# Token rows kept in plain feature order, and every eighth feature taken as stationary columns on TensorE

## The chip, the core and the metric

The kernel runs on one core of a Trainium2 chip. The metric is the device time of one execution in microseconds (us); lower is better. The engines are TensorE (PE in the profile; its weight loads have a row of their own, PEld), VectorE (DVE), ScalarE (ACT), GpSimd (POOL) and SyncE (SP), which issues most of the DMAs.

## The reference

The model has two layers over 256 tokens of `x` and, in layer 0, 256 tokens of context as well, with 1024 features. Each layer is a mixer (two kinds of attention in layer 0, one in layer 1) with its output projection, a residual and layer norm, then a mixture of 16 experts, of which every token takes 2, and another residual and layer norm.

```python
x = layer_norm(ALPHA * x + g1 * y, ln_g[l, 0], ln_b[l, 0])
h2 = x * (1.0 + sc2) + sh2
x = layer_norm(ALPHA * x + g2 * moe(h2, ...), ln_g[l, 1], ln_b[l, 1])

def moe(h, w_router, b_router, w_gate, w_up, w_down):
    scores = jax.nn.sigmoid(h @ w_router)
    ...                                   # best of 4 groups, its 2 best experts, gates
    g = jnp.einsum('...d,edf->...ef', h, w_gate)
    u = jnp.einsum('...d,edf->...ef', h, w_up)
    a = jax.nn.silu(g) * u * gates[..., None].astype(h.dtype)
    return jnp.einsum('...ef,efd->...d', a, w_down)
```

`w_gate` and `w_up` have 1024 x 512 values per expert, `w_down` 512 x 1024. All of it is fp32.

## The kernel before

Tokens lie in tiles of 128 partitions: four tiles in layer 0 (two of `x`, two of context), two in layer 1. `out_proj` closes each mixer. For every tile it multiplies the attention output with the output weights (L855), adds the residual on VectorE (L857, L858), takes the statistics for the layer norm, and computes the router's logits on TensorE (L872, L877). The reciprocal root of the variance is a power on GpSimd (`rstd`, L370). Two VectorE instructions then make the row `h2` that the experts see: one subtracts the mean and multiplies with a row (L887), the other multiplies with the reciprocal root and adds a row (L894). The scores are made beside them (L890, L891, L893, L901, L902). Behind the last tile the routing begins (`route_a`, `route_b`), a long chain of small VectorE instructions.

The feature order matters because of the expert weights. `w_gate` and `w_up` are loaded so that partition p holds the features 8p to 8p + 7, in eight slices k; slice k of the weights therefore holds every eighth feature, starting with k. The transposed tokens that are multiplied with slice k must hold the same features. Before the change `h2` is written in that order: L887 reads its inputs in order and writes feature 8q + k to column 128k + q, and L894 reads and writes in that permuted order. Neighbouring elements of the write are thus 512 bytes apart.

Layer 0: `h2` is stored to `h2d` in DRAM by a DMA on ScalarE's queue (L897). For each block of 128, 64 or 32 tokens of an expert, GpSimd gathers rows into `xg` (L1207) and `xgT` transposes them on TensorE, eight transposes for the eight slices of 128 columns. In a transpose the data is the stationary operand, loaded by a weight load, and the identity is the moving one; `tr` is the helper of all transposes (L234). VectorE or ScalarE copies the result to `xt` (L1223), `products` multiplies it with gate and up weights (L1232, L1234 for 128 tokens, L1247 for fewer), `hidden` makes the activation, `down` the down product (L1284, L1290). There are 20 blocks, so 160 transposes.

Layer 1: `h2` stays in SBUF as `h2s`, split into two fp32r parts, the cast (L899, ScalarE) and what the cast leaves (L900, VectorE). `pick` takes the tokens of a group of blocks out of it with one-hot matrices `ddr`: for each of eight slices, two tiles and two parts one matmul with 128 columns of `h2s` as the stationary operand and up to 128 one-hot columns as the moving one (L1311); ScalarE copies the result (L1313). There are seven groups, so 7 x 8 x 2 x 2 = 224 such matmuls.

Expert weights come through rings of buffers on SyncE's queue (L155), each load waiting until its buffer is free.

Of the kernel before, what the change touches and what calls it, by code (L numbers as in the profile page):

```python
# [14 lines left out]
ALU = mybir.AluOpType  # L15
# [6 lines left out]
P = 128  # L22
# [120 lines left out]
class K:  # L143
# [698 lines left out]
    def out_proj(self, l, ts, w, oT, rows, h2d, score):  # L842
        nc, wk = self.nc, self.wkb
        for n, t in [(n, t) for n in range(2) for t in ts]:
            c = t // 2
            g1, G2, B2 = [rows[:, 3 * c + i] for i in range(3)]
            cs = slice(512 * n, 512 * n + 512)
            zs = []
            if n:
                zs.append(self.half_T(self.xs[:, t, 0:512], 0))  # L850
                bs = self.sm.tile([P, 2, 6], F32, name="bs", tag="bs")
                nc.vector.bn_stats(bs[:, 0], self.xs[:, t, 0:512])
            ps = self.psum([P, 512], "acc")
            for k in range(8):
                mm = nc.tensor.matmul(ps, oT[:, k, P * t:P * t + P], w[n](k), start=k == 0, stop=k == 7)  # L855
            y = wk.tile([P, 512], F32, name="y", tag="yw")
            nc.vector.tensor_mul(y, ps, g1[:, cs])  # L857
            nc.vector.scalar_tensor_tensor(self.xs[:, t, cs], self.xs[:, t, cs], ALPHA if l == 0 else 1.0, y,  # L858
                                           op0=ALU.mult, op1=ALU.add)
            if n == 0:  # L860
                continue

            last = t == ts[-1]
            if last:
                w0 = self.warm(7, "m", mm.ins.name)
            zs.append(self.half_T(self.xs[:, t, 512:1024], 1))
            nc.vector.bn_stats(bs[:, 1], self.xs[:, t, 512:1024])
            wg, bl = self.router
            pr = self.psum([P, P], "tr")
            for k in range(8):  # L870
                j = k % 4
                nc.tensor.matmul(pr[32 * j:32 * j + 32, :], wg[:, c, k, :], zs[k // 4][:, j, :], start=k < 4, stop=k > 3,  # L872
                                 tile_position=(0, 32 * j), skip_group_check=True)
            lp = wk.tile([P, P], F32, name="lp", tag="lp", bufs=1)
            nc.scalar.copy(lp, pr)
            ps = self.psum([P, NE], "tr")
            self.routed = nc.tensor.matmul(ps, lp, self.const("sum4"), start=True, stop=True).ins.name  # L877
            mv = self.sm.tile([P, 6], F32, name="mv5", tag="mv5")
            nc.vector.bn_aggr(mv[:, 0:2], bs)
            self.rstd(mv[:, 2:3], mv[:, 1:2], 1, 1e-5)  # L880
            nc.vector.tensor_scalar(mv[:, 3:4], mv[:, 0:1], -1.0, None, op0=ALU.mult)

            z = self.xs[:, t, :]
            h2 = wk.tile([P, D], F32, name="h2", tag="h2")

            hq, rq = "p (k q) -> p q k", "p (q k) -> p q k"
            nc.vector.scalar_tensor_tensor(h2.rearrange(hq, k=8), z.rearrange(rq, k=8), mv[:, 0:1], G2.rearrange(rq, k=8),  # L887
                                           op0=ALU.subtract, op1=ALU.mult)
            sc = score[:, t, :]
            nc.vector.scalar_tensor_tensor(sc, bl[:, c, 1], mv[:, 3:4], ps, op0=ALU.mult, op1=ALU.add)  # L890
            nc.vector.scalar_tensor_tensor(sc, sc, mv[:, 2:3], bl[:, c, 0], op0=ALU.mult, op1=ALU.add)  # L891

            e = nc.scalar.activation(sc, sc, AF.Exp, scale=-1.0)  # L893
            nc.vector.scalar_tensor_tensor(h2.rearrange(hq, k=8), h2.rearrange(hq, k=8), mv[:, 2:3], B2.rearrange(rq, k=8),  # L894
                                           op0=ALU.mult, op1=ALU.add)
            if l == 0:
                nc.scalar.dma_start(h2d[P * t:P * t + P, :], h2)  # L897
            else:
                nc.scalar.copy(self.h2s[0][:, t], h2)  # L899
                nc.vector.tensor_sub(self.h2s[1][:, t], h2, self.h2s[0][:, t])  # L900
            nc.vector.tensor_scalar(sc, sc, 1.0, None, op0=ALU.add)  # L901
            nc.vector.reciprocal(sc, sc)  # L902
            nc.vector.tensor_mul(mv[:, 4:5], mv[:, 3:4], mv[:, 2:3])
            nc.scalar.activation(z, z, AF.Identity, scale=mv[:, 2:3], bias=mv[:, 4:5])
            if last:
                i = nc.scalar.activation(self.junk, self.nhalf[:, 0:1], AF.Sigmoid)
                self.tc.add_manual_dep(i.ins, e.ins.name, NOSYNC, reason="behind the exponentials")
# [302 lines left out]
    def scatter(self, y, si, R, yd, NT):  # L1210
        nj = P // R
        self.nc.gpsimd.indirect_dma_start(out=yd.rearrange("r (j w) -> (r j) w", j=nj), out_offset=IOA(ap=si, axis=0),
                                          in_=y, in_offset=None, bounds_check=2 * NT * nj - 1, oob_is_err=False)

    def xgT(self, xg, R):
        nc = self.nc
        xt = self.ep.tile([P, 8, R], F32, name="xt", tag="xt")
        kb = min(8, 512 // R)
        for k0 in range(0, 8, kb):
            pt = self.psum([P, kb, R], "tr")  # L1220
            for k in range(kb):
                self.tr(pt[:, k, :], xg[:R, P * (k0 + k):P * (k0 + k) + P], R)
            nc.any.tensor_copy(xt[:, k0:k0 + kb, :], pt)  # L1223
        return xt

# [72 lines left out]
    def pick(self, dd, T):  # L1298

        nc = self.nc  # L1300
        R = dd.shape[2]
        xt = self.ep.tile([P, 8, R], F32, name="xt", tag="xt")
        kb = min(8, 512 // R)
        for k0 in range(0, 8, kb):
            n = min(kb, 8 - k0)
            pt = self.psum([P, n, R], "tr")
            for k in range(n):
                ks = slice(P * (k0 + k), P * (k0 + k) + P)
                for t in range(T):
                    for i in range(2):  # L1310
                        nc.tensor.matmul(pt[:, k, :], self.h2s[i][:, t, ks], dd[:, t, :],  # L1311
                                         start=t == 0 and i == 0, stop=t == T - 1 and i == 1)
            nc.any.tensor_copy(xt[:, k0:k0 + n, :], pt)  # L1313
        return xt
# [572 lines left out]
```

## Time and profile before

| what | us |
|---|---|
| median of three runs | 1063.53 |
| their range | 1056.98 to 1065.07 |
| the profiled execution | 1061.43 |
| its span in the trace | 1059.6 |

The span is the time from the first to the last recorded instruction of the profiled execution; what lies around it makes the difference to that execution's time. An engine's busy time says how long it had work, not whether that work decided the end. Of TensorE the trace shows two rows, the weight loads (PEld) and the matmuls (PE); a load can run while the matmul ahead of it still runs. Waits are read from the idle time ahead of an instruction and from what released it.

### The profile page before, as it was taken

The numbers are of one execution on the slowest core, as the hardware profiler recorded it, in microseconds if no ns is written. First come the engines' busy times: TensorE is split into PE (matmuls) and PEld (weight loads), VectorE is DVE, ScalarE is ACT, GpSimd is POOL, SyncE is SP. The second block draws the span as 40 slices with busy tenths as digits, with TensorE's granted clock in tenths as the row PEclk, the third lists the DMA queues.
The fourth block names the chain that finished last, engine by engine and source line by source line (L and its number), as shares of the span: only waits on it lengthen the run. The fifth ranks groups of instructions, "written<-read, shape, count | busy, mean of one in ns | idle before, by whom it ended". The sixth has DMA issues, their size and how long they took to land. (4 is left out here: it accounts for less than half of the span.)

```text
span 1059.6 us, 15578 instructions
## 1 busy us (share of the span) xinstructions
PE 979.2 (92%) x5918; PEld 533.2 (50%) x5918; DVE 507.3 (48%) x1368; ACT 259.9 (25%) x685; POOL 86.0 (8%) x90
## 2 busy tenths in 40 slices
PE   4799999989899899999999997998999999999994
PEld 1466557667544444544444443443653665544542
DVE  2524555665747833331100105879838742533346
ACT  2433343553412111101111211423413111111110
POOL 0000000000102303111111110111003000000001
PEclk9799999999999999999999899999999889999997
DMA  8899761201265199997999986769634692999991
GB/s 313 298 350 330 258 214 58 80 24 57 105 239 214 63 392 401 408 414 292 390 402 401 358 301 248 315 245 405 263 140 136 252 418 79 417 418 376 363 353 47
DMA packets 76937, 286.99 MB, mean 271 GB/s; under 512 B 12449, under 2 KB 27441, under 8 KB 55604
## 3 DMA queue, kind: packets, MB, share of 16 engines
q1 hardware_dynamic: 71600, 268.13, 65.4%
q0 software_dynamic: 4272, 15.08, 4.0%
q10 hardware_dynamic: 980, 2.66, 0.6%
q8 instruction: 51, 0.84, 0.3%
q14 instruction: 34, 0.28, 0.1%
HBM read 279.77 MB, written 8.69 MB: 272 GB/s over the span
## 5 line engine op out<-in xcount | busy, mean ns | idle before, releaser
L1247 PE MATMUL acc<-wring,xt 128*32 128x256 f32 (+1 forms) x1440 | 140.2, 436 | 0.5 <-ACT xt L1223 0.5
L1247 PEld LDWEIGHTS acc<-wring,xt 128*32 128x32 f32 (+1 forms) x1440 | 59.0, 118 | 73.1 <-issue 49.7
L855 PE MATMUL acc<-wring,oT 128*128 128x512 f32 x192 | 89.2, 598 | 0.3 <-DVE y L857 0.3
L1290 PE MATMUL acc<-wring,aT 128*32 128x256 f32 (+1 forms) x720 | 70.7, 436 | 6.5 <-DVE aT L1272 4.2
L459 PE MATMUL acc<-swh,hT 128*128 128x384 f32 x192 | 68.2, 355 | 3.9 <-ACT v L581 3.5
L460 PE MATMUL acc<-swl,hT 128*128 128x384 f32 x192 | 67.6, 352 | 0.0
L1349 DVE TENSOR_TENSOR xs<-xs,c 128x512 f32<-128x512 f32 x60 | 40.4, 684 | 54.6 <-PE c L1346 54.5
L461 PE MATMUL acc<-swh,hT 128*128 128x384 f32 x192 | 66.2, 345 | 0.0
L523 PE MATMUL acc<-wring,hT 128*128 128x512 f32 x128 | 58.8, 593 | 0.0
L1284 PE MATMUL acc<-wring,aT 128*128 128x512 f32 x128 | 57.1, 597 | 0.5 <-DVE aT L1261 0.4
L1232 PE MATMUL acc<-wring,xt 128*128 128x512 f32 x128 | 56.7, 596 | 0.0
L1234 PE MATMUL acc<-wring,xt 128*128 128x512 f32 x128 | 56.2, 592 | 0.0
L410 PE MATMUL m<-wring,cT 128*32 128x512 f32 x256 | 44.3, 660 | 12.4 <-DMA wring<-in_w_mod_dram 12.4
L855 PEld LDWEIGHTS acc<-wring,oT 128*128 128x128 f32 x192 | 33.9, 190 | 33.0 <-issue 31.4
L1290 PEld LDWEIGHTS acc<-wring,aT 128*32 128x32 f32 (+1 forms) x720 | 27.8, 117 | 38.1 <-issue 20.7
L370 POOL TENSOR_TENSOR mv<-ve,nhalf 128x1 f32<-128x1 f32 x12 | 18.3, 1529 | 330.9 <-DVE ve L369 263.6
L1250 ACT COPY gu<-acc 128x256 f32<-128x256 f32 (+1 forms) x27 | 12.0, 444 | 122.5 <-PE acc L1247 122.5
L459 PEld LDWEIGHTS acc<-swh,hT 128*128 128x128 f32 x192 | 36.4, 189 | 9.5 <-issue 4.5
L1234 PEld LDWEIGHTS acc<-wring,xt 128*128 128x128 f32 x128 | 24.3, 190 | 30.6 <-issue 30.4
L1232 PEld LDWEIGHTS acc<-wring,xt 128*128 128x128 f32 x128 | 23.8, 190 | 28.3 <-issue 27.6
L461 PEld LDWEIGHTS acc<-swh,hT 128*128 128x128 f32 x192 | 36.3, 189 | 3.0 <-issue 3.0
L460 PEld LDWEIGHTS acc<-swl,hT 128*128 128x128 f32 x192 | 36.4, 190 | 2.4 <-issue 2.4
(354 smaller groups left out, 1527.9 us busy)
## 6 DMA issues: line engine op xcount, KB each, us to landing
wring<-in_w_gate_dram SPq DMA_DIRECT2D x58, 1024.0 KB, 14.4
wring<-in_w_up_dram SPq DMA_DIRECT2D x58, 1024.0 KB, 15.3
wring<-in_w_down_dram SPq DMA_DIRECT2D x58, 1024.0 KB, 14.2
wring<-in_w_mod_dram SPq DMA_DIRECT2D x48, 1024.0 KB, 8.1
wring<-in_w_in_even_dram SPq DMA_DIRECT2D x24, 256.0 KB, 4.4
wring<-in_w_in_odd_dram SPq DMA_DIRECT2D x6, 1024.0 KB, 11.4
wring<-in_w_out_even_dram SPq DMA_DIRECT2D x4, 1024.0 KB, 5.1
wring<-yd SPq DMA_DIRECT2D x4, 1024.0 KB, 5.8
```

The costliest lines, as they stand in the source:

```text
L410: nc.tensor.matmul(ps[32 * j:32 * j + 32, :], lhs(k), w[k][:, 512 * j:512 * j + 512], start=k == 0, stop=k == len(w) - 1, tile_position=(0 ...
L459: mm(ps, xh, wh, start=first, stop=False)
L460: mm(ps, xh, wl, start=False, stop=False)
L461: mm(ps, xl, wh, start=False, stop=last)
L523: self.nc.tensor.matmul(ps, h[:, k, :], w(k), start=k == 0, stop=k == 7)
L855: mm = nc.tensor.matmul(ps, oT[:, k, P * t:P * t + P], w[n](k), start=k == 0, stop=k == 7)
L1232: nc.tensor.matmul(pg, xt[:, k, :], gate(k), start=k == 0, stop=k == 7)
L1234: nc.tensor.matmul(pu, xt[:, k, :], up(k), start=k == 0, stop=k == 7)
L1247: nc.tensor.matmul(ps[R * j:R * j + R, :], xt[:, k, :], src[:, W * jj:W * jj + W], start=k == 0, stop=k == 7, tile_position=(0, R * j), sk ...
L1284: nc.tensor.matmul(ps, aT[:, k, :], w(k)[:, 512 * n:512 * n + 512], start=k == 0, stop=k == 3)
L1290: self.last_mm = nc.tensor.matmul(ps[R * j:R * j + R, :], aT[:, k, :], w(k)[:, W * j:W * j + W], start=k == 0, stop=k == 3, tile_position= ...
L1349: nc.vector.tensor_add(x, x, ps)
```

## The change

`h2` is now written in plain feature order: the two VectorE instructions of each tile read and write side by side. The features are picked where the rows go into TensorE: a new helper `eighth` views a row as 128 groups of eight and takes the k-th of each, and `xgT` and `pick` use this view as their stationary operand. Its columns stand eight elements (32 bytes) apart instead of side by side. What comes out of the transposes and picks is the same as before, in the same place.

```diff
-            hq, rq = "p (k q) -> p q k", "p (q k) -> p q k"
-            nc.vector.scalar_tensor_tensor(h2.rearrange(hq, k=8), z.rearrange(rq, k=8), mv[:, 0:1], G2.rearrange(rq, k=8),
-                                           op0=ALU.subtract, op1=ALU.mult)
+            nc.vector.scalar_tensor_tensor(h2, z, mv[:, 0:1], G2, op0=ALU.subtract, op1=ALU.mult)
...
-            nc.vector.scalar_tensor_tensor(h2.rearrange(hq, k=8), h2.rearrange(hq, k=8), mv[:, 2:3], B2.rearrange(rq, k=8),
-                                           op0=ALU.mult, op1=ALU.add)
+            nc.vector.scalar_tensor_tensor(h2, h2, mv[:, 2:3], B2, op0=ALU.mult, op1=ALU.add)
...
+    def eighth(self, x, k):
+        return x.rearrange("p (q k) -> p k q", k=8)[:, k]
...
-                self.tr(pt[:, k, :], xg[:R, P * (k0 + k):P * (k0 + k) + P], R)
+                self.tr(pt[:, k, :], self.eighth(xg[:R, :], k0 + k), R)
...
-                ks = slice(P * (k0 + k), P * (k0 + k) + P)
                 for t in range(T):
                     for i in range(2):
-                        nc.tensor.matmul(pt[:, k, :], self.h2s[i][:, t, ks], dd[:, t, :],
+                        nc.tensor.matmul(pt[:, k, :], self.eighth(self.h2s[i][:, t], k0 + k), dd[:, t, :],
```

Every engine keeps its instructions in the same order. In the instruction lists only twelve rows of VectorE differ, two for each of the six token tiles, and they differ in shape alone (128 x 128 x 8 before, 128 x 1024 now). The gathers, the stores to `h2d` and the weight loads from DRAM are as before, and the numbers of transposes and picks too. A path for experts with more tokens than planned uses the same two functions.

## Rows read from the trace of the kernel before

**Rows 1.** The page's first part, TensorE's busy time, share and instructions.
```profile
PE 979.2 (92%) x5918; PEld 533.2 (50%) x5918; DVE 507.3 (48%) x1368; ACT 259.9 (25%) x685; POOL 86.0 (8%) x90
```
**Rows 2.** Five stretches: length, busy time by engine, granted clock, DMA share, GB/s.
```profile
318.00:356.00 38.00, 36.67 (x172) 16.55 (x171) 29.75 (x54) 10.75 (x20) 10.34 (x6) 0.96 0.43 173
...
370.00:480.00 110.00, 107.56 (x691) 52.41 (x684) 38.27 (x102) 13.89 (x29) 16.37 (x14) 0.99 1.00 402
480.00:626.00 146.00, 145.24 (x974) 66.39 (x972) 13.07 (x28) 24.40 (x52) 19.61 (x20) 0.98 0.93 364
...
821.00:827.00 6.00, 5.95 (x40) 5.25 (x40) 2.11 (x16) 0.96 (x2) 0.00 (x0) 0.70 0.36 91
```
**Rows 3.** TensorE's waits, 365 to 625 us: in total, times, longest.
```profile
PE tr L234 <- DMA xg<-h2d,ix: 2.0, 2, 1.2
```
**Rows 4.** Waits of SyncE's DMA queue, 365 to 625 us.
```profile
SPq L155 <- PE acc L1290: 62.6, 13, 17.1
```
**Rows 5.** TensorE's waits, 815 to 1047 us.
```profile
PE acc L1290 <- DVE aT L1272: 3.9, 7, 1.0
```
**Rows 6.** L234 from 365 to 625 us: durations in ns, least, median, most; forms.
```profile
L234 PEld LDWEIGHTS tr<-ident,xg x160: 133/138/143, 367.8 to 618.5; 32*128 32x128 f32 x80, 128*128 128x128 f32 x48, 64*128 64x128 f32 x32
...
L234 PEld LDWEIGHTS tr<-ident,G x1: 87/87/87, 597.6 to 597.6; 128*16 128x16 f32 x1
```
**Rows 7.** The same view of L1247, weight loads of 32 columns mostly.
```profile
L1247 PEld LDWEIGHTS acc<-wring,xt x1440: 106/110/230, 369.0 to 1036.6; 128*32 128x32 f32 x144, 128*64 128x64 f32 x36
```
**Rows 8.** Timeline of weight loads, 365 to 625 us: start, length, instruction, count.
```profile
407.94 0.57 PEld L234 LDWEIGHTS tr<-ident,xg 32*128 32x128 f32 x8
...
420.19 0.85 PEld L234 LDWEIGHTS tr<-ident,xg 128*128 128x128 f32 x8 [1.08 <-DMA xg<-h2d,ix]
430.49 0.91 PEld L234 LDWEIGHTS tr<-ident,xg 128*128 128x128 f32 x8
```
**Rows 9.** L1311, the picks: durations of the weight loads in ns.
```profile
L1311 PEld LDWEIGHTS tr<-ddr,h2s x224: 186/192/338, 821.1 to 985.8; 128*128 128x128 f32 x112
```
**Rows 10.** Timeline of weight loads, 820 to 1000 us.
```profile
821.05 4.83 PEld L1311 LDWEIGHTS tr<-ddr,h2s 128*128 128x128 f32 x32 [1.04 <-DVE ddr L1366]
...
890.96 3.43 PEld L1311 LDWEIGHTS tr<-ddr,h2s 128*128 128x128 f32 x30 [0.24 <-issue]
```
**Rows 11.** Durations of L887, L1635, L1131 and L1109 on VectorE, in ns.
```profile
L887 DVE SCALAR_TENSOR_TENSOR h<-xs,mv,mid x6: 1977/1997/2011, 322.6 to 807.3; 128x1024 f32<-128x1024 f32 x6
...
L1635 DVE SCALAR_TENSOR_TENSOR xs<-xs,lnB x2: 1216/1217/1218, 828.9 to 830.0; 128x1024 f32<-128x1024 f32 x2
...
L1131 DVE TENSOR_TENSOR big<-PM,cst x2: 443/444/446, 375.6 to 844.3; 128x169 f32<-128x169 f32 x2
...
L1109 DVE TENSOR_TENSOR big<-PM,o x4: 336/336/337, 369.3 to 373.8; 128x169 f32<-128x169 f32 x4
```
**Rows 12.** Timeline, last tile of layer 0.
```profile
349.77 1.98 DVE L887 SCALAR_TENSOR_TENSOR h<-xs,mv,mid 128x1024 f32<-128x1024 f32 x1
349.87 2.16 POOL L370 TENSOR_TENSOR mv<-ve,nhalf 128x1 f32<-128x1 f32 x1 [6.85 <-DVE mv L881]
...
351.59 0.21 DVE L890 SCALAR_TENSOR_TENSOR score<-bl,mv,tr 128x16 f32<-128x16 f32 x1
...
352.07 1.98 DVE L894 SCALAR_TENSOR_TENSOR h<-h,mv,mid 128x1024 f32<-128x1024 f32 x1 [0.27 <-POOL mv L370]
```
**Rows 13.** Timeline, the final layer norm.
```profile
1049.66 1.28 DVE L1851 SCALAR_TENSOR_TENSOR xs<-xs,mv,wring 128x1024 f32<-128x1024 f32 x1
1049.83 1.52 POOL L370 TENSOR_TENSOR mv<-ve,nhalf 128x1 f32<-128x1 f32 x1 [230.49 <-DVE ve L369]
```
**Rows 14.** Timeline, first tile of layer 1's output projection and the next.
```profile
800.56 3.60 PE L855 MATMUL acc<-wring,oT 128*128 128x512 f32 x8
...
803.28 1.23 DVE L900 TENSOR_TENSOR h2s<-h,h2s 128x1024 fp32r<-128x1024 f32 x1 [0.71 <-ACT h2s L899]
...
804.80 0.63 DVE L857 TENSOR_TENSOR y<-acc,mid 128x512 f32<-128x512 f32 x1
```

## The prediction

> **What bounds the kernel now.** I read the page's busy line first: TensorE is busy for 979.2 of 1059.6 us [rows 1]. A share like that says little alone, because the ends of matmuls are modelled, so I looked at the stretches that the change touches [rows 2] and asked in each what TensorE waits for. Layer 0's experts run from about 370 to 626 us. There TensorE is busy 107.56 of 110 us and 145.24 of 146 us, its longest wait in total is 2.0 us for gathered rows [rows 3], and the queue that loads weights waits for TensorE: 62.6 us for the down products alone [rows 4]. The DMA share of 1.00 looks like a second bound, but the waiting goes from the loads to TensorE, not back. Layer 1's experts, 821 to 1047 us, read the same: TensorE's longest wait in total is 3.9 us, for VectorE [rows 5]. So both expert stages are a queue of TensorE work with little slack, and a microsecond added to that queue is nearly a microsecond at the end. The output projection, 318 to 356 us, is TensorE's too (36.67 of 38 us busy), up to its last tile, where a short chain over VectorE and GpSimd decides when routing can begin.
>
> **What the change takes away.** Twelve VectorE instructions, two for each of six token tiles, lose their far-apart access. The first reads in order and writes every element 512 bytes from the last; it takes 1.997 us, and an instruction of the same kind and size in plain order takes 1.217 us [rows 11]. Each saves 0.78 us, 9.4 us of VectorE time in all. The first three tiles of layer 0 hide theirs behind TensorE's matmuls of the next tile. What counts is three places.
>
> (a) The last tile of layer 0 [rows 12]. GpSimd's power (the reciprocal root of the variance) starts 0.1 us behind the first VectorE instruction and ends 0.28 us after it, having taken 2.16 us; the second starts right then. At the kernel's end the same power, beside a plain instruction of 1.28 us, takes 1.52 us [rows 13]. So the power gets shorter with its neighbour and ends at about 351.4 instead of 352.03. That isn't all won: the score instruction stands ahead of the second one on VectorE and waits for the router's product; it began at 351.59 and could hardly begin before 351.45. I take 0.4 us, plus 0.78 us on the second instruction, behind which the scores and the routing stand: 1.2 us.
>
> The trace shows the power lengthened beside VectorE. The Trainium skill, "SBUF — State Buffer", section "SBUF: two separate sides", has a rule for it: an instruction of VectorE with two SBUF inputs and one of GpSimd that reads SBUF take a shared port pair in turn, each for its whole length. By that rule the whole difference of the two rows, 0.64 us, would pass on to the power; the sum above gives 0.4 us of it because of the score instruction, and by the rule alone it would be 0.2 us better.
>
> (b) The last tile of layer 1: the same chain, 1.2 us. (c) The first tile of layer 1 [rows 14]: TensorE ends that projection at 804.16 us, but the next tile's first VectorE instruction (the product with the gate row, L857) begins at 804.80, since it is queued behind the subtraction of L900, which waits for the cast of the strided result. With that chain over a microsecond earlier TensorE's end decides again: 0.6 us. Together **3.0 us saved**.
>
> **What the change adds.** No instruction is added, and none changes its place on any queue. What changes is where 384 weight loads of TensorE read: their columns stand 32 bytes apart instead of side by side. 160 are the loads of layer 0's transposes of gathered rows: 48 for blocks of 128 rows, 32 for 64, 80 for 32 [rows 6]. 224 are the loads of layer 1's picks [rows 9]. Are loads what these stretches wait for? Eight loads of a 32-row block take 0.57 us, so one starts every (0.57 - 0.14)/7 = 61 ns; those of a 128-row block every (0.85 - 0.14)/7 = 101 ns, up to 110 ns in others of these blocks, where the 128 moving rows set the pace [rows 8]. A load of 128 columns lasts 138 ns and one of 16 columns 87 ns [rows 6], which makes 0.455 ns a column or 58 ns for 128: nearly all of the 61. So the loads set the pace for 112 of the 160. For the picks, 30 loads take 3.43 us, one each (3.43 - 0.19)/29 = 112 ns [rows 10]. A load lasts 192 ns [rows 9], and one of the same precision with 32 columns 110 ns [rows 7]: 0.85 ns a column, 109 ns for 128. So every pick goes at the pace of its load.
>
> What a column 32 bytes on costs in such a load no row shows: in the trace of before all stationary operands lie side by side. The low end is nothing. The nearest rows are VectorE's. There a product over 169 elements takes 336 ns when both inputs lie in order and 444 ns when one is read 52 bytes apart [rows 11]: 0.64 ns more an element; writing apart costs 0.76 ns more an element by L887. In both forms VectorE's time an element grows by a bit over a half. I take for TensorE that **the time a column takes doubles**, which is 0.455 ns more in a transpose and 0.85 ns more in a pick, on either side of VectorE's 0.64. Then:
> - transposes of 64 and 32 rows: 112 x 58 ns = 6.5 us;
> - transposes of 128 rows: 61 + 58 = 119 ns for the load against 110 now, 48 x 9 ns = 0.4 us;
> - picks: 192 x 109 ns = 20.9 us, and the first 32, at a granted clock of 0.70 [rows 2], spaced (4.83 - 0.19)/31 = 150 ns and so 1.34 times as long: 32 x 109 x 1.34 = 4.7 us.
>
> That is 32.5 us. With VectorE's 0.64 ns added to each column instead, 82 ns a load, it is 9.2 + 1.6 + 19.2 = 30.0 us; the choice between the two matters little. Nothing covers it: what could is a wait of TensorE, and those come to a few microseconds in both stages [rows 3, 5]. Net **+29.5 us**.
>
> The Trainium skill, "SBUF — State Buffer", section "Door 1: The DMA port swizzle", speaks against this change: it says that reads need at least two hits in each 16-byte line for full bandwidth, and that each step to a new line pays. At 32 bytes every column is a new line, in fp32. It gives no price, and no run before this one shows TensorE under it; by it the sum keeps its sign, and VectorE's two rows agree.
>
> **Rivals.**
> 1. *The loads are free at any step.* TensorE may be fed from far-apart columns as fast as from neighbours; nothing in the trace forbids it, VectorE's rows speak against it. Then only the 3.0 us remain: 1061.43 - 3.0 = 1058.4, not slower than before. It decides if a strided load of 128 columns lasts under about 145 ns in a transpose and 200 ns in a pick.
> 2. *Only the transposes pay.* A pick's load takes 0.85 ns a column already, about twice a transpose's; if that is a second step on a column already read, a slower read hides in it. Then 6.9 - 3.0: 1065.3. For it: the two slopes differ by nearly two; against: nothing shows what the second step is.
> 3. *A hop costs TensorE as long as VectorE.* VectorE needs 1.217/1024 = 1.19 ns an element in order and 1.19 + 0.64 = 1.83 apart, in its own time. At 1.83 ns a column a load takes 234 ns: transposes of 64 and 32 rows go from 61 to 237 ns (19.7 us), those of 128 from 110 to 237 (6.1 us), picks from 112 to 237, 125 ns x (192 + 32 x 1.34) = 29.4 us. Less 3.0: 1113.6.
> 4. *A pick reads each column twice, each at that price.* Picks go to 471 ns, 359 x 235 = 84 us; in all about 1168. It needs two dear assumptions at once.
>
> **How the numbers follow.** The sum stands on the profiled execution, 1061.43 us, of which the span is 1059.6; the median of the three runs is 1063.53, 0.2% above, and a median of the changed kernel may lie as much above the sum. Forecast: 1061.43 + 29.5 = 1090.9, say 1091. Chances: doubled columns 0.44, rival 1 0.12, rival 2 0.16, rival 3 0.18, rival 4 0.10. The range runs from rival 1 to a little past rival 3, 1058 to 1115, and leaves out rival 4. Within 1% (which is about what a measurement of this kernel can tell from no change, as three runs spread by 0.8%) lie rivals 1 and 2 and a cheap form of the forecast: 0.30. Faster by over 1% would take 10 us where 3 are to be had: 0.02. Slower: 0.68.
>
> **What would show it.** In the profile of the changed kernel: the two VectorE instructions at about 1.22 us; GpSimd's power beside them at about 1.5; the weight loads of gathered rows at about 195 ns instead of 138, eight in a 32-row block over 0.97 us instead of 0.57; those of the picks at about 300 ns and spaced 220; TensorE's waits unchanged, layer 0's experts some 7 us longer and layer 1's some 25. Loads of unchanged length make rival 1 true, 138 to 195 beside an unchanged 192 rival 2, and about 310 ns for both kinds rival 3. I would be wrong in another way if TensorE turned out to be waiting for weights inside groups that look busy: then the added time would be covered in part, and the end would move by less than the loads do.

## The result

The changed kernel takes 1102.58 us (median of four runs, 1099.2 to 1104.51); the kernel before, with a fourth run added, takes 1060.26. The ratio is 1.0408, with a 95% interval of 1.0374 to 1.0441: slower. The forecast was 1091, with a range of 1058 to 1115. The direction and the range held; the increase was 42 us where 29.5 had been worked out, so the sum lacks some 13 us.

The page of the changed kernel, first part, answers to [rows 1]:

```profile
span 1102.3 us, 15578 instructions
...
PE 1026.2 (93%) x5918; PEld 571.1 (52%) x5918; DVE 499.5 (45%) x1368; ACT 259.8 (24%) x685; POOL 82.5 (7%) x90
```

The span grew by 42.7 us and TensorE's busy time by 47.0; VectorE's fell by 7.8. No waits were added: TensorE's longest wait in layer 1's experts, from the view of waits between 825 and 1090 us, is what it was in [rows 5].

```profile
PE acc L1290 <- DVE aT L1272: 3.8, 6, 1.0
```

**Where the time went, by stage.** Each stage is taken from the start of its first to the start of its last piece of TensorE work. In the timeline of the kernel before, layer 0's experts run from the first transpose to the matmuls of L212 behind the last down product, and layer 1's from the first pick [rows 10] to the last matmul of L1346:

```profile
367.85 0.65 PE L234 MATMUL tr<-ident,xg 32*128 32x32 f32 x8 [1.15 <-DMA xg<-h2d,ix]
...
635.99 4.27 PE L212 MATMUL acc<-onesb,identb 128*128 128x512 bf16 x19
...
1045.62 0.28 PE L1346 MATMUL c<-yl,dt 128*128 128x256 f32 x1
```

The same places in the timeline of the changed kernel:

```profile
365.62 1.04 PE L234 MATMUL tr<-ident,xg 32*128 32x32 f32 x8 [1.00 <-DMA xg<-h2d,ix]
...
641.59 4.49 PE L212 MATMUL acc<-onesb,identb 128*128 128x512 bf16 x20
...
825.44 7.89 PE L1310 MATMUL tr<-ddr,h2s 128*128 128x96 f32 x32 [0.57 <-DVE ddr L1365]
...
1088.33 0.28 PE L1345 MATMUL c<-yl,dt 128*128 128x256 f32 x1
```

Layer 0's experts went from 268.1 to 276.0 us, +7.8; layer 1's from 224.6 to 262.9, +38.3. With the 3.0 us saved elsewhere (below) that is 43.1, and the span moved by 42.7. So the loss sits in the two stages that were named, but layer 1's is half as large again as the 25 us that were forecast for it.

**The loads.** Durations in ns (least, median, most) of the transposes' weight loads and of the picks', and three groups of the timeline of weight loads, all of the changed kernel; they answer to [rows 6, 8 to 10]:

```profile
L234 PEld LDWEIGHTS tr<-ident,xg x160: 180/199/207, 365.6 to 624.1; 32*128 32x128 f32 x80, 128*128 128x128 f32 x48, 64*128 64x128 f32 x32
L1310 PEld LDWEIGHTS tr<-ddr,h2s x224: 312/336/341, 825.4 to 1026.5; 128*128 128x128 f32 x112
```

```profile
406.55 0.95 PEld L234 LDWEIGHTS tr<-ident,xg 32*128 32x128 f32 x8
...
418.45 0.97 PEld L234 LDWEIGHTS tr<-ident,xg 128*128 128x128 f32 x8
...
908.79 7.70 PEld L1310 LDWEIGHTS tr<-ddr,h2s 128*128 128x128 f32 x31 [0.24 <-issue]
```

A transpose's load lasts 199 ns (195 forecast), and in a 32-row block one starts every (0.95 - 0.20)/7 = 107 ns, against 61 before. A 128-row block has one every 110 ns, within the 101 to 110 of before. A pick's load lasts 336 ns (300 forecast), and one starts every (7.70 - 0.336)/30 = 245 ns, against 112; 221 had been forecast.

**The savings** came as worked out. Timeline of the changed kernel, last tile of layer 0; it answers to [rows 12]:

```profile
349.03 1.27 DVE L885 SCALAR_TENSOR_TENSOR h<-xs,mv,mid 128x1024 f32<-128x1024 f32 x1
349.14 1.57 POOL L370 TENSOR_TENSOR mv<-ve,nhalf 128x1 f32<-128x1 f32 x1 [7.46 <-DVE mv L881]
350.64 0.23 DVE L887 SCALAR_TENSOR_TENSOR score<-bl,mv,tr 128x16 f32<-128x16 f32 x1 [0.33 <-PE tr L877]
350.79 1.28 DVE L891 SCALAR_TENSOR_TENSOR h<-h,mv,mid 128x1024 f32<-128x1024 f32 x1
```

The two VectorE instructions take 1.27 and 1.28 us instead of 1.98, GpSimd's power beside them 1.57 instead of 2.16, and the second one now starts right behind the score instruction, which waits for TensorE. The first instruction and the second start 1.76 us apart, where they were 2.30, so 0.54 us was won up to there and 0.70 behind it: 1.24 for the 1.2 forecast. For layer 1's first tile, the step from one L857 to the next went from 9.64 to 9.04 us: the 0.6 forecast.

**What the loads don't explain.** The 192 later picks at 133 ns more are 25.5 us; the first 32, which take 7.73 us where [rows 10] have 4.83, add 2.9; and picks among other matmuls pay less, since part of their load lies beside those. That is 28 us at most, of the 38.3. The rest stands in the work behind the picks, and the granted clock shows why. Windows of layer 1's experts, first of the kernel before, then of the changed one with four stretches round the picks at 908.8 (columns as in [rows 2]):

```profile
821.00:1047.10 226.10, 216.90 (x1648) 122.03 (x1648) 102.77 (x259) 28.93 (x61) 0.00 (x0) 0.97 0.79 314
```

```profile
825.40:1089.80 264.40, 255.53 (x1648) 152.14 (x1648) 103.31 (x258) 28.99 (x61) 0.00 (x0) 0.90 0.68 269
908.80:912.80 4.00, 4.00 (x18) 3.88 (x17) 1.44 (x2) 0.62 (x1) 0.00 (x0) 1.00 0.00 0
912.80:916.60 3.80, 3.80 (x16) 3.68 (x17) 0.00 (x0) 0.59 (x1) 0.00 (x0) 0.73 0.00 0
916.60:920.60 4.00, 4.00 (x11) 1.24 (x12) 0.43 (x1) 0.59 (x1) 0.00 (x0) 0.50 0.00 0
920.60:926.10 5.50, 5.50 (x25) 1.62 (x22) 0.00 (x0) 0.00 (x0) 0.00 (x0) 0.93 0.45 134
```

TensorE is busy all through this burst of picks, yet the granted clock falls within it from 1.00 (the 2.4 GHz level) to 0.50 (the 1.2 GHz level), and the work behind the burst starts there. Timeline of TensorE, the first product groups behind two bursts, kernel before and then the changed one:

```profile
894.46 7.09 PE L1247 MATMUL acc<-wring,xt 128*64 128x512 f32 x32
...
928.88 7.09 PE L1247 MATMUL acc<-wring,xt 128*64 128x512 f32 x32
```

```profile
908.81 7.86 PE L1310 MATMUL tr<-ddr,h2s 128*128 128x128 f32 x31
...
916.60 9.45 PE L1247 MATMUL acc<-wring,xt 128*64 128x512 f32 x32
...
957.30 9.58 PE L1247 MATMUL acc<-wring,xt 128*64 128x512 f32 x32
```

The same 32 matmuls take 7.09 us before and 9.45 or 9.58 now. Six groups of gate and up products lie behind bursts of picks; they take 1.7, 1.6, 2.4, 2.5, 2.5 and 1.9 us more, 12.6 in all.

The whole stage can be divided in this way. In the trace TensorE's matmuls start one after another, so the time from one start to the next can be put down to the first of the two and summed by kind. The kernel before and the changed one, and two variants that follow below, in us:

| layer 1's experts | before | changed | `pick_twice` | `pick_warm` |
|---|---|---|---|---|
| picks | 29.0 | 54.2 | 56.7 | 56.2 |
| added matmuls | | | | 16.1 |
| gate and up products | 95.3 | 108.8 | 96.9 | 93.1 |
| everything else | 100.3 | 99.9 | 99.3 | 100.1 |
| stage | 224.6 | 262.9 | 252.9 | 265.5 |

So the 38.3 us are 25.2 of picks and 13.5 of products, whose own instructions didn't change, and nothing else grew.

Two theories went to the chip. **Theory A**: the loads cost about 28 us, and some 10 more come from the clock, which falls because long bursts of slow loads with few moving columns stand in a row. **Theory B**: the clock isn't what costs, and the whole loss belongs to the loads or is lost elsewhere. What B would show differs from one experiment to the next, and each expectation says it anew.

### The profile page after: what moved, and what is told of

It reads as the page before. It is cut to its first block, busy times and chain, and to the rows that moved or that the text cites. A ratio compares the mean times of both kernels' runs of the same rounds, so it can differ in the third digit from the quotient of the medians.

```text
span 1102.3 us, 15578 instructions
## 1 busy us (share of the span) xinstructions
PE 1026.2 (93%) x5918; PEld 571.1 (52%) x5918; DVE 499.5 (45%) x1368; ACT 259.8 (24%) x685; POOL 82.5 (7%) x90
## 5 line engine op out<-in xcount | busy, mean ns | idle before, releaser
L1247 PE MATMUL acc<-wring,xt 128*32 128x256 f32 (+1 forms) x1440 | 150.9, 457 | 0.5 <-ACT xt L1223 0.5
L1247 PEld LDWEIGHTS acc<-wring,xt 128*32 128x32 f32 (+1 forms) x1440 | 61.9, 123 | 81.2 <-issue 59.2
L1232 PE MATMUL acc<-wring,xt 128*128 128x512 f32 x128 | 60.3, 626 | 0.0
L1310 PE MATMUL tr<-ddr,h2s 128*128 128x128 f32 (+1 forms) x224 | 57.9, 413 | 0.6 <-DVE ddr L1365 0.6
L1310 PEld LDWEIGHTS tr<-ddr,h2s 128*128 128x128 f32 x224 | 55.8, 334 | 4.5 <-issue 3.1
L1234 PE MATMUL acc<-wring,xt 128*128 128x512 f32 x128 | 56.2, 592 | 0.0
L370 POOL TENSOR_TENSOR mv<-ve,nhalf 128x1 f32<-128x1 f32 x12 | 14.7, 1228 | 371.5 <-DVE ve L369 302.4
L459 PEld LDWEIGHTS acc<-swh,hT 128*128 128x128 f32 x192 | 36.8, 192 | 9.5 <-issue 4.5
L1232 PEld LDWEIGHTS acc<-wring,xt 128*128 128x128 f32 x128 | 25.2, 202 | 30.4 <-issue 29.9
```

What stands on the lines that cost most here:

```text
L459: mm(ps, xh, wh, start=first, stop=False)
L1232: nc.tensor.matmul(pg, xt[:, k, :], gate(k), start=k == 0, stop=k == 7)
L1234: nc.tensor.matmul(pu, xt[:, k, :], up(k), start=k == 0, stop=k == 7)
L1247: nc.tensor.matmul(ps[R * j:R * j + R, :], xt[:, k, :], src[:, W * jj:W * jj + W], start=k == 0, stop=k == 7, tile_position=(0, R * j), sk ...
L1310: nc.tensor.matmul(pt[:, k, :], self.eighth(self.h2s[i][:, t], k0 + k), dd[:, t, :], start=t == 0 and i == 0, stop=t == T - 1 and i == 1)
```

## The experiments

The variants give each layer a number of neighbouring features, `b`, that stay together in the token row: 8 is the changed kernel's plain order (columns 32 bytes apart in the load), 4 leaves columns 16 bytes apart, 2 leaves 8, and 1 is the order of before (side by side). `eighth` picks its columns accordingly. All variants differ from this frame by little:

```
+    RUN = (8, 8)                      # b of layer 0, of layer 1
+    def eighth(self, x, k, l):
+        b = self.RUN[l]
+        return x.rearrange("p (a q b) -> p a b q", b=b, a=8 // b)[:, k // b, k % b]
```

**One layer at a time.** `tr_only` has plain order in layer 0 alone (strided transposes, picks as before), `pick_only` in layer 1 alone.

```
tr_only:    RUN = (8, 1)
pick_only:  RUN = (1, 8)
```

> Layer 0 as in the changed kernel (plain rows, strided transposes), layer 1 as before (permuted rows, picks side by side). Theory A (strided loads cost, and in layer 1 the clock that falls behind long strided picks costs about 10 us more): the transposes' 112 short loads go from 61 to 107 ns, +5 us, the tail of layer 0 gives back 1.2, a little clock: +4 to +8 us. Theory B (loads alone, the rest of the 42 us is lost in layer 0 and in waits there): +12 us or more.

> Layer 0 as before, layer 1 as in the changed kernel (plain rows, strided picks). Theory A: picks go from 112 to 245 ns, +28 us, clock +10, tail of layer 1 -1.8: +34 to +38 us, mean granted clock of layer 1's expert stage about 0.90. Theory B: +26 us, as the loads alone make it.

`tr_only` measured 1064.01 us, ratio 1.0023 [0.9996, 1.0049]; layer 0's experts take 273.0 us, +4.9, and layer 1's picks 192 ns again. The ratio makes 2.4 us, a little under A's +4 to +8, and far from B's +12. `pick_only` measured 1096.94, ratio 1.0339 [1.0287, 1.0391], with the whole growth of layer 1, as A had it: its picks take 54.1 us and its products 108.7. Its windows and the group behind the burst:

```profile
818.10:1082.50 264.40, 255.44 (x1648) 151.94 (x1648) 103.37 (x259) 29.06 (x61) 0.00 (x0) 0.90 0.68 269
```

```profile
909.27 9.45 PE L1264 MATMUL acc<-wring,xt 128*64 128x512 f32 x32
```

The two ratios make 1.036 together, just under the 1.0374 at which the interval of the whole change begins. So the loss is the picks'; the transposes cost a few microseconds, of which the savings give most back. Layer 0's stage grew by 7.8 us in the whole change and by 4.9 here with the same loads. Divided as above, the transposes take 5.5 and 5.2 us more than before, nearly the same. The windows of this stage in the kernel before, the changed one and `tr_only` have a granted clock of 0.98, 0.97 and 0.98, so the 3 us between them go with the clock; with one profile of each, whether they belong to the change stays open.

**The same load time without slow loads.** `pick_twice` is the kernel before with every pick made a second time from a fresh start. It has 448 loads of 192 ns instead of 224 of 336, so about the same added load time and twice the moving columns.

```
+                for r in range(2):
                     for t in range(T):
                         for i in range(2):
                             nc.tensor.matmul(pt[:, k, :], ...)
```

> The kernel before with every pick made twice (the second from a fresh start, so the result stays): 448 loads side by side at 112 ns, nearly the time of 224 strided ones at 245, but twice the columns through TensorE. Theory A (the clock falls because few columns flow through while strided loads run): +25 us, the granted clock of layer 1's expert stage stays at about 0.97. Theory B (the clock falls for the length of the picks or by chance): clock as low as 0.90 and +35 us.

It measured 1089.91 us, ratio 1.0263 [1.0208, 1.0317]. Its windows and timeline:

```profile
822.00:1076.40 254.40, 245.34 (x1872) 149.81 (x1872) 102.72 (x258) 29.06 (x61) 0.00 (x0) 0.96 0.71 279
```

```profile
903.00 7.55 PE L1328 MATMUL tr<-ddr,h2s 128*128 128x128 f32 x63
...
910.48 7.09 PE L1264 MATMUL acc<-wring,xt 128*64 128x512 f32 x32
```

TensorE's queue of loads is 149.81 us busy here and 151.94 in `pick_only`; the burst at 903 lasts nearly as long as that at 908.81 above. But the clock is 0.96, not 0.90, the groups behind bursts take 7.09 us (all but one, 8.50), and the stage is 10.0 us shorter. By the sums of starts its picks take even 2.6 us more than `pick_only`'s, and its products 11.8 less. Its time is 28 us over the kernel before, between A's +25 and B's +35 and nearer to A. So equal time on loads doesn't make the clock fall so far, and where it stays up some 12 us are not lost. It isn't safe from falling, though: in one of its six bursts ahead of products (60 picks, 941.64 to 950.32 us, mean clock 0.77) it fell as well, and that is the group of 8.50 us.

**The clock held up.** `pick_warm` is `pick_only` with one matmul of 512 bf16 columns behind each pick, whose result nobody reads.

```
+        wm = self.psum([P, 512])
...
+                        nc.tensor.matmul(wm, self.identb, self.onesb[:, None, :].to_broadcast([P, 4, P]), start=True, stop=True)
```

> The strided picks of pick_only, with a matmul of 512 bf16 columns behind each, whose result nobody reads, while the next strided load runs. Theory A (the clock falls because few columns flow through while strided loads run, and the work behind the picks pays): granted clock of layer 1's expert stage 0.95 or more, pace of a pick 245 to 290 ns, time within 4 us of pick_only although 224 matmuls of over 200 ns are added, and the expert groups behind the picks back at their time of before (L1247 of 32 matmuls at 7.1 us). Theory B (the clock falls for the strided reads themselves): clock stays at 0.90, those groups at 9.5 us, and 10 us or more slower than pick_only.

It measured 1099.76 us, ratio 1.037 [1.0333, 1.0407]. Its windows, and three groups of TensorE's timeline:

```profile
818.40:1085.50 267.10, 258.31 (x1871) 161.73 (x1870) 103.12 (x259) 29.02 (x61) 0.00 (x0) 0.99 0.67 266
```

```profile
854.74 3.91 PE L1330 MATMUL acc<-onesb,identb 128*128 128x512 bf16 x16
...
863.38 3.66 PE L1264 MATMUL acc<-wring,xt 128*32 128x256 f32 x64
...
954.96 7.09 PE L1264 MATMUL acc<-wring,xt 128*64 128x512 f32 x32
```

The loads still last 312 to 341 ns, so they are as slow as in `pick_only`; the clock is back at 0.99, and all the groups behind bursts at their times of before (3.66 and 7.09 us). The added matmuls pay for themselves only in part. 35 of them had been moved off their picks into rows of their own, at some 0.22 us each (16 from 854.74 to 858.29), and the others space their picks by about 0.30 us instead of 0.245: 8 + 10 = 18 us of work. The stage grew by 2.7 over `pick_only`, so some 15 us came back. The table has them in the products: 93.1 us, 15.6 less than in `pick_only` and even 2.2 less than in the kernel before, which loses a little to the clock too. Of A's forecast only the pace of a pick, 300 ns, lies outside (245 to 290). The clock's price is real, then: 13.5 us against the kernel before, with 11.8 won back in `pick_twice` and 15.6 in `pick_warm`. Theory B falls.

**Nearer columns.** `pairs` keeps two features together in both layers, so that the loads' columns are 8 bytes apart, `quads` four, 16 bytes apart. The two VectorE instructions become four and two shorter ones.

```
pairs:  RUN = (2, 2)
quads:  RUN = (4, 4)
+            for a in range(8 // b):       # n = 128 * b
+                h = h2[:, n*a:n*a + n].rearrange("p (q b) -> p q b", b=b)
+                x = z.rearrange("p (q a b) -> p a q b", b=b, a=8 // b)[:, a]
```

> Rows in an order that keeps two neighbouring features together, so that VectorE reads and writes in pairs (four instructions of 256 elements in place of one of 1024) and TensorE's stationary columns stand 8 bytes apart in both layers. If a load pays for each step to a new 16-byte line without a second hit: loads as before, 138 and 192 ns, and only VectorE's gain is left, -1 to -3 us against before. If any step costs as much as 32 bytes do: +40 us, as the changed kernel. If VectorE pays for pairs too: loads fast, but no gain, 0.

> Runs of four features, columns 16 bytes apart in both layers. If a line of 16 bytes must be hit twice for a fast pick: picks as at 32 bytes, 336 ns a load, layer 1 38 us longer, total +40 us. If the price rises with the distance: between 196 and 336 ns, +10 to +30 us. Transposes about 200 ns a load in any case, as at 8 and 32 bytes.

`pairs` measured 1064.38 us, ratio 1.0055 [1.0024, 1.0087]: slower, if by little, and none of its three outcomes came whole, since the picks went at the pace of before and the transposes didn't. Loads of its transposes and picks (ns), the timeline of its weight loads, and GpSimd's power at layer 0's last tile:

```profile
L234 PEld LDWEIGHTS tr<-ident,xg x160: 189/211/221, 364.9 to 620.9; 32*128 32x128 f32 x80, 128*128 128x128 f32 x48, 64*128 64x128 f32 x32
L1327 PEld LDWEIGHTS tr<-ddr,h2s x224: 193/196/222, 821.8 to 986.7; 128*128 128x128 f32 x112
```

```profile
364.87 1.03 PEld L234 LDWEIGHTS tr<-ident,xg 32*128 32x128 f32 x8 [1.08 <-issue]
...
891.08 3.63 PEld L1327 LDWEIGHTS tr<-ddr,h2s 128*128 128x128 f32 x30 [0.23 <-issue]
```

```profile
348.69 1.67 DVE L886 SCALAR_TENSOR_TENSOR h<-xs,mv,mid 128x256 f32<-128x256 f32 x4
348.80 0.77 POOL L370 TENSOR_TENSOR mv<-ve,nhalf 128x1 f32<-128x1 f32 x1 [8.27 <-DVE mv L881]
```

`quads` measured 1101.66, ratio 1.0388 [1.0337, 1.044], the first of its two outcomes. The same two views of its picks, and one block of its transposes:

```profile
L1327 PEld LDWEIGHTS tr<-ddr,h2s x224: 307/330/338, 820.4 to 1020.9; 128*128 128x128 f32 x112
```

```profile
363.01 1.03 PEld L234 LDWEIGHTS tr<-ident,xg 32*128 32x128 f32 x8 [1.08 <-issue]
...
903.29 7.53 PEld L1327 LDWEIGHTS tr<-ddr,h2s 128*128 128x128 f32 x31 [0.24 <-issue]
```

Time from one load to the next in a burst, worked out as above:

| columns apart | 4 bytes | 8 | 16 | 32 |
|---|---|---|---|---|
| transposes, 32 rows (ns) | 61 | 117 | 117 | 107 |
| picks (ns) | 112 | 118 | 240 | 245 |

The price is a step, not a slope, and the two kinds take it at different places: the transposes lose already at 8 bytes, the picks only at 16. So the picks of `pairs` are nearly free, and its layer 1 stage is 224.7 us, as before; its loss is in layer 0, whose experts take 273.5 us, 5.4 more.

**A version that might beat both.** `l1_pairs` leaves layer 0 as before and takes pairs in layer 1, where VectorE's gain comes without a loss on TensorE.

```
l1_pairs:  RUN = (1, 2)
```

> Layer 0 as before (its transposes paid for pairs too), layer 1 with pairs, whose picks went at the pace of before: layer 1's tail 3.5 us shorter, nothing added: -2 to -4 us against before. If what pairs lost lay in layer 1 as well, 0 or slower.

It measured 1061.88 us in twelve runs, ratio 1.002 [0.9993, 1.0048]: no gain, and not the forecast. Its timeline behind the last tile of layer 1:

```profile
807.40 0.19 DVE L960 TENSOR_TENSOR sel<-score,brow 128x32 f32<-128x32 f32 x1
...
808.53 1.22 DVE L898 TENSOR_TENSOR h2s<-h,h2s 128x1024 fp32r<-128x1024 f32 x1
...
815.57 3.93 PEld L1327 LDWEIGHTS tr<-ddr,h2s 128*128 128x128 f32 x32 [1.53 <-DVE ddr L1382]
```

The routing's first instruction comes 6.65 us behind the tile's L857, where it took 9.52 before: 2.9 us won. Then 1.4 are lost: the subtraction of 1.22 us (L898 here, L900 before), which stood ahead of the routing, now stands in the middle of it, and the first pick comes 8.17 us after that instruction instead of 6.73. What is left in this profile, 1.5 us plus the first tile's 0.6, is 0.2% of the kernel. The interval ends at 0.07% faster, so the runs don't show even that; what takes it back stays open.

## Why the prediction was right in direction and too small

- *What bounds the kernel* held. Waits in both expert stages are as before, and added load time came out at the end nearly whole: 25.2 us in the picks and 5.5 in the transposes.
- *What the change takes away* held in all three places: 1.24, 1.19 and 0.6 us, 3.0 together, and with the reason given: the power of 2.16 us takes 1.57 beside instructions of 1.27, and 0.77 beside the quarter-length ones of `pairs`. It ends 0.28, 0.40 and 0.40 us behind the VectorE instruction that it started beside. The Trainium skill, "SBUF — State Buffer", section "SBUF: two separate sides", has GpSimd wait out a whole VectorE instruction with two SBUF inputs if both read SBUF; the power's three lengths agree.
- *What the change adds, transposes*: 6.9 us forecast; 112 x 46 = 5.2 and next to nothing for 128 rows by the spacings, 5.5 by the sum of starts, +4.9 in `tr_only`'s stage. Right, if a little dear.
- *What the change adds, picks*: 20.9 + 4.7 = 25.6 us forecast, 25.2 measured, but partly by luck. In a burst the column's time more than doubled, 133 ns a load where 109 was taken, which would make 25.5 us for the 192; they paid 22.3, mostly since picks that stand among other matmuls pay less. The first 32 got a factor 1.34 for a lower clock and 4.7 us; they paid 2.9, and the reason for the factor was wrong. Strided loads start at the same pace at either clock level (see the last section), while side-by-side ones fell from 18 in 2 us at 1.00 to 13 at 0.57: the lower clock had already slowed the loads of before, so there was less to lose.
- *"Nothing covers it: ... Net +29.5 us"* is the step that failed. It looked only for cover, and counted the loads as if the work behind them stayed the same. The clock of that work is a term of its own, left at nothing: 13.5 us in layer 1, shown from two sides by `pick_twice` and `pick_warm`. The other terms as measured, 25.2 + 5.5 - 3.0 = 27.7 us, lie close to the 29.5; with the clock's 13.5 they make 41.2, where 42 were measured. The range held because rival 3 had stretched it upwards, for another reason.
- *The rivals*: free loads and "only the transposes pay" fell by the rows of loads; what the second says does happen with columns 8 bytes apart, in `pairs`. "A hop costs TensorE as long as VectorE" asked for about 310 ns in both kinds; 199 and 336 came. It came as near in time as the forecast, 11 us too slow where that was 12 too fast, but only because its dearer transposes stood in for the clock. The picks at 471 ns fell too.
- *Two hits in each 16-byte line*, the rule of the Trainium skill, "SBUF — State Buffer", section "Door 1: The DMA port swizzle", fits the picks: 118 ns with two columns in 16 bytes, 240 with one. For the transposes it doesn't hold: 117 ns with two columns in 16 bytes, twice the 61 of four.

## What to carry to other kernels

A stationary operand should be laid out so that its columns lie side by side, or at least measured at the distance in question. Here the re-ordering on VectorE cost 3 us at the end, and was hidden behind TensorE for three of the six tiles; the 384 strided loads cost 31, and the clock behind them 13.5. Where TensorE is the bound, added time in bursts of short matmuls must be priced twice: for itself, and for the clock at which the work behind it starts; the granted clock just behind such bursts in the profile tells. An off-path instruction that finishes sooner on a busy queue can slip from ahead of a critical chain into it, as in `l1_pairs`.

## What the runs showed of the hardware

- The time from one weight load of 128 fp32 columns to the next goes by the columns' distance in one step, at 8 bytes for transposes (61 to 117 ns) and at 16 bytes for the picks (118 to 240). Why the two differ stays open, and so does why 32 bytes are a little cheaper than 8 or 16 for transposes (107 against 117).
- The pace of strided loads didn't change with the granted clock: one started every 239 ns (median) at 1.00 and at 0.50. That of neighbouring columns did: 112 ns at 1.00 and 213 at 0.50, in the kernel before and in `pick_twice`. Windows of the changed kernel with the picks alone (PE, PEld, granted clock):

```profile
910.80:912.80 2.00, 2.00 (x10) 2.00 (x10) 1.00 0.00 0
...
829.50:831.50 2.00, 2.00 (x10) 2.00 (x10) 0.50 0.00 0
```

The same of the kernel before, its first 32 picks:

```profile
821.10:823.10 2.00, 2.00 (x18) 2.00 (x19) 1.00 0.90 210
823.10:825.10 2.00, 2.00 (x13) 2.00 (x12) 0.57 0.12 42
```

- TensorE fell to its lower clock level without a gap in its records: a burst of 31 picks with loads of 336 ns began at 1.00 and ended at 0.50, whereas 63 picks with loads of 192 ns, in nearly the same time, left the group behind them at its full speed (7.09 us). It happened in all six bursts ahead of products in the changed kernel, in one of six in `pick_twice`, and in none in `pick_warm`, where matmuls of 512 columns stand among the slow loads.
